# Attention's gate fourteen to seventeen steps later, the first merged set built in its output tiles, and a last pair of operands that is not sent to memory

## The chip, the cores and the metric

One core of a Trainium2 chip runs the whole layer. TensorE (PE) multiplies, VectorE (DVE) and ScalarE (ACT) work on the elements, GpSimd (POOL) and SyncE (SP) issue DMA transfers in their program's order. An engine runs its own list of instructions in order, and waits for others by semaphores. The metric is the device time of one execution in microseconds, the median of several; smaller is better.

## The reference

A bidirectional encoder layer on 768 tokens (512 and 256) of width 2048, all in float32. What is left out here are the modulation by `c`, the norms and the pooling windows.

```
proj = h @ w_in                       # 2048 -> 10240
pool_u, pool_z, q, k, v, attn_z, g_pool, g_attn = split(proj)
pool_y = _pool_mixer(pool_u) * silu(pool_z)
attn_y = _neighbourhood_attention(rms(q), rms(k), v, rpb) * silu(attn_z)   # the gate
merged = sigmoid(g_pool) * (pool_y @ w_pool_up) + sigmoid(g_attn) * (attn_y @ w_attn_up)
return x + gate * (merged @ w_o)
```

## The kernel before

Activations lie transposed: 128 features on the partitions, 768 tokens along the row, as a tile of 128 x 2 x 384 floats (384 KB). A weight or an activation is split in a rounded high part and the rest, and a product is three matmuls (high x high, high x low, low x high). Weights `wraw` are loaded by SP, split by ACT (`whi`, line 378) and DVE (`wlo`, line 379), three pieces ahead of PE.

Most products go by Strassen's scheme in Winograd's form: a *set* of activations (XA, XB, XR, XY, MA, MB, each with 4 *pairs* of tiles) is held as seven operands (B11, T1, T2, B21, T3, T4, B22) of each pair, and a *job* of seven products in 14 *steps* gives two output tiles `o1` and `o2` (line 490, 12 matmuls a product). A step is a place in the order in which the program is written, `clock["now"]`; everything that is not PE's main work is put into that order by `at(step, fn)`, or waits in one of three lists that `pump` serves once a step: `tasks` (loads that bring operands back), `back` (making a set's operands), `chores`.

`store` makes a set: `fetch` loads a pair of tiles (`in`) on SP, then `put` casts an operand on ACT (line 200) and subtracts on DVE (line 204), `differ` and `differ_too` make the differences on DVE (lines 284 to 290), and `save` sends an operand to memory on POOL (line 254). `recall` brings operands back on POOL (line 320). Operands named in `keep` stay. They lie in 46 slots of the slab, and `heap` counts those in use; a slot counts as free four steps after its save was issued, and who takes it next waits for the real landing. The tiles that jobs give lie in a ring of 7 buffers, the pool `outs`.

In the middle of the run eight pairs of heads go through attention beside the jobs of XB. A pair takes 42 steps, in six *units* of 7: scores, softmax, a transpose of the probabilities (`pt`, split by ACT into `ph` and by DVE into `pl`, line 697), and a product with v, whose tiles are transposed by PE first (`vt`, line 657). The gate, silu(attn_z), comes with the last unit: it loads `az`, takes exp, adds 1, takes log and exp again, and multiplies twice. The step is counted from the last unit's start, and the next pair starts 7 steps after that:

```python
stages += [(2, gate_load), (7, gate_exp), (8, gate_sum), (9, gate_log), (10, gate_inv), (12, gate_mul), (15, gated)]
```

After XB come eight jobs with XR (the pooled branch), eight with XY (attention, `au_done`), and eight each with MA and MB, the merged activations of features 0 to 1023 and 1024 to 2047, times `w_o`. In a job of XY each output tile is multiplied by its sigmoid gate `sig` (lines 962 to 966), gets the pooled branch added by an accumulating DMA (`o<-mp_d`, line 981), and goes to memory as `merged_d` (line 984). MA is made from `merged_d` while XY's jobs run, MB while MA's jobs run. In MA's jobs `x` is added by an accumulating DMA (line 995) and the sum goes to `half_d` (line 1001).

Of the kernel before, what the change touches and what calls it, by code (L numbers as in the profile page):

```python
# [44 lines left out]
PAIRS = 4  # L45
# [6 lines left out]
def encoder_layer(ctx: ExitStack, tc: tile.TileContext, xT, cT, w_ada2, w_ada4, b_ada, norm_g, w_in, pool_w,  # L52
# [37 lines left out]
    def release(t, n):  # L90
        if not any(t is o for o in outs.get("own", ())):
            after(n, free)

    def flat(t):
        return t.rearrange("p h n -> p (h n)")
# [48 lines left out]
    clock = {"now": 0}  # L144
# [48 lines left out]
    class Set:  # L193
# [3 lines left out]
        def put(self, op, j, src, then=None):  # L197

            t = self.ops[op, j] = slot(f"{self.name}{op}", F32R)
            act.copy(t[:, 0, :], src)  # L200
            flush()

            def rest():
                dve.tensor_tensor(t[:, 1, :], src, t[:, 0, :].bitcast(F32), op=ALU.subtract)  # L204
                if then is not None:
                    then()

            behind["fn"] = rest
            behind["of"] = t
# [30 lines left out]

    RAW = {"B11": ("a", 0), "B12": ("a", 1), "B21": ("b", 0), "B22": ("b", 1)}

    def store(st, load, ready=lambda j: True, make=None, last=None, keep=(), ahead=False):

        got = [{} for _ in range(st.pairs)]

        def fetch(j):
            got[j]["a"], got[j]["b"] = load(j)
            got[j]["t"] = clock["now"]

        def save(op, j):
            t = st.ops.pop((op, j))
            st.saved[op, j] = d = dram.tile([P, 2, TH], F32R, name=f"{st.name}{op}{j}")
            pool.dma_start(d, t)

            def landed():
                free()
                heap["flying"] -= 1
            after(4, landed)

        def put(op, j, src, then=None):
            kept = op in keep
            heap["flying"] += not kept

            def done():
                if then is not None:
                    then()
                if not kept:
                    save(op, j)

            st.put(op, j, src, done)
            mine = behind["of"]
            after(2, lambda: flush() if behind and behind["of"] is mine else None)

        def free_slot(op):
            return lambda: op in keep or heap["flying"] < heap["fly"] or hurry["on"]

        def here(j):
            return clock["now"] >= got[j]["t"] + 6 or hurry["on"]

        def differ(j):
            a, b = got[j]["a"], got[j]["b"]
            flush()
            dve.tensor_tensor(a[:, 0, :], a[:, 0, :], a[:, 1, :], op=ALU.subtract)
            dve.tensor_tensor(a[:, 1, :], b[:, 1, :], a[:, 1, :], op=ALU.subtract)

        def differ_too(j):
            a, b = got[j]["a"], got[j]["b"]
            dve.scalar_tensor_tensor(b[:, 1, :], a[:, 0, :], -1.0, b[:, 1, :], op0=ALU.mult, op1=ALU.subtract)
            dve.scalar_tensor_tensor(b[:, 0, :], b[:, 1, :], -1.0, b[:, 0, :], op0=ALU.mult, op1=ALU.subtract)  # L290

        def fetches(j):
            back.append((2, lambda: ready(j) and free_slot("")(), lambda: fetch(j)))

        def pair(j):
            if j == 0 or not ahead:
                fetches(j)
            if make is not None:
                for k in "ab":
                    back.append((0, lambda: here(j), lambda k=k: make(j, k, got[j][k])))  # L300
            for op in ("B22", "B21", "B11"):
                k, h = RAW[op]
                back.append((1, lambda op=op: here(j) and free_slot(op)(), lambda op=op, k=k, h=h: put(op, j, got[j][k][:, h, :])))
            back.append((0, lambda: True, lambda: differ(j)))
            back.append((0, lambda: True, lambda: differ_too(j)))
            if ahead and j + 1 < st.pairs:
                fetches(j + 1)
            for op, k, h, then in (("T3", "a", 1, None), ("T4", "b", 0, None), ("T1", "a", 0, free), ("T2", "b", 1, free)):
                back.append((1, free_slot(op), lambda op=op, k=k, h=h, then=then: put(op, j, got[j][k][:, h, :], then)))
            if j == st.pairs - 1 and last is not None:  # L310
                back.append((0, lambda: True, lambda: after(6, last)))

        for j in range(st.pairs):
            pair(j)

    def recall(st, keep=()):

        def load(op, j):
            t = st.ops[op, j] = slot(f"{st.name}{op}", F32R)
            pool.dma_start(t, st.saved[op, j])  # L320

        for op in ORDER:
            for j in range(0 if op not in keep else st.pairs, st.pairs):
                tasks.append((1, lambda op=op, j=j: (op, j) in st.saved, lambda op=op, j=j: load(op, j), 1))

    hurry = {"on": False}

# [271 lines left out]
    def attention(p, start, pace):  # L599
# [4 lines left out]
        def unit_(u):  # L604
# [148 lines left out]
            stages = [(-6, fetch), (0, scores), (1, biased), (3, exps), (5, vtrans), (6, vsplit), (5, recip), (6, norm),  # L753
                      (9, ptrans), (10, psplit), (13, values), (14, out)]
            if u == 5:
                stages += [(2, gate_load), (7, gate_exp), (8, gate_sum), (9, gate_log), (10, gate_inv), (12, gate_mul), (15, gated)]
            for d, fn in stages:
                if new or fn not in (vtrans, vsplit):
                    at(start + pace * u + d, fn)
# [218 lines left out]
    def au_done(f):  # L978
        def go(i, t):
            gate_with(16 + f, t)  # L980
            pool.dma_start(flat(t), mp_d[f], accum_op=ALU.add)

            def out():
                pool.dma_start(merged_d[f], flat(t))
                state.setdefault("merged", set()).add(f)
                release(t, 3)
            after(5, out)
        return go

# [230 lines left out]
    def stored(src, f):  # L1220
        got = []
        for i in range(2):
            t = slot("in")
            sp.dma_start(flat(t), src[f + i])
            got.append(t)
        return got

    with tc.tile_pool(name="attn", bufs=1, reuse_waits="tile") as at_:
        state["pool"] = at_
        act.preload_act_table_set(LNEXP)  # L1230
        now = clock["now"]
        first = now + 25
        for p in range(8):
            attention(p, first, 7 if p < DENSE else 8)
            first += 42 if p < DENSE else 56
        done = first + 14 - now
        heap["fly"] = 1
        store(XR, lambda j: stored(pooled_d, 2 * j))
        store(XY, lambda j: stored(attn_d, 2 * j), lambda j: state.get("gated", -1) >= 2 * j + 1)
        run(done)  # L1240
# [7 lines left out]
        sig_load(f)  # L1248
    recall(XY)
    run(14 + 14 * 8 + 2)  # L1250
    kept = ("B11", "T1", "T2")
    heap["gap"] = 2
    for k, st in enumerate((MA, MB)):
        store(st, lambda j, k=k: stored(merged_d, 8 * k + 2 * j),
              lambda j, k=k: {8 * k + 2 * j, 8 * k + 2 * j + 1} <= state.get("merged", set()), keep=kept, ahead=True)
        recall(st, kept)
        run(8 * 14)
    run(8 * 14 - 2)
# [91 lines left out]
```

## Time and profile before

| | |
|---|---|
| median of 3 runs | 2034.09 us (2033.81 to 2039.09) |
| the profiled execution | 2040.75 us, its span 2039.0 us |
| PE busy | 1925.6 us, 94% of the span |
| DVE, ACT, POOL busy | 66%, 51%, 19% |
| mean granted clock of TensorE | 0.972 |

The span runs from the first to the last instruction. PE works nearly all the time, so what a change is worth stands in the stretches where PE waits or runs at the lower of its two clock levels (1.2 in place of 2.4 GHz, a granted clock of 0.50). At the full clock PE does 232 matmuls of 384 columns in 40 us, 5.8 in a microsecond, so a job of 84 takes 14.5 us and a step 1.03 us.

### The profile page before, as it was taken

What the parts mean: (1) busy time and instruction counts of PE and PEld (TensorE: products, weight loads), DVE (VectorE), ACT (ScalarE), POOL (GpSimd) and SP (SyncE); (2) the same over time, 40 slices, a digit from 0 to 9 for tenths busy, and PEclk for the clock granted to TensorE, in tenths of its full rate; (3) what the DMA queues carried; (4) which work ended last, traced back from release to release, by engine and by line L of the source; (5) the groups of instructions that cost most, each with busy time, mean ns of one, the idle gap of its engine ahead of it and who ended that gap; (6) DMA issues with size and microseconds to landing.
All of it is one profiled execution on the core that took longest, in us unless ns stands there. A gap on an engine that the chain in (4) does not pass through costs nothing.

```text
span 2039.0 us, 32071 instructions
## 1 busy us (share of the span) xinstructions
PE 1925.6 (94%) x11752; PEld 1816.6 (89%) x11752; DVE 1354.6 (66%) x2422; ACT 1029.7 (51%) x2224; POOL 388.9 (19%) x617
## 2 busy tenths in 40 slices
PE   4899999999999999999999999999999997988997
PEld 2788889898999999999888988898999997888997
DVE  5755556666655588776687667777767776766654
ACT  4433334444434354456566666666545444554553
POOL 0000000111200256411111111111231222322311
PEclk8999999999999999999899999999999998989999
DMA  9755556887733645565656565556798789989965
GB/s 351 247 196 184 199 192 227 271 259 242 263 133 129 209 109 150 143 176 152 164 129 177 139 165 154 145 153 150 229 354 288 228 262 291 313 259 263 279 184 143
DMA packets 133774, 423.20 MB, mean 208 GB/s; under 512 B 16880, under 2 KB 22000, under 8 KB 133616
## 3 DMA queue, kind: packets, MB, share of 16 engines
q0 software_dynamic: 64352, 203.72, 36.5%
q1 hardware_dynamic: 68256, 217.35, 31.9%
q8 instruction: 92, 1.51, 0.3%
q14 instruction: 66, 0.54, 0.1%
q10 hardware_dynamic: 1008, 0.09, 0.0%
HBM read 296.83 MB, written 124.26 MB: 207 GB/s over the span
## 4 chain that ended last, share of the span: by engine, by line
PE 80%; DMA 6%; DVE 6%; issue 4%; ACT 3%; POOL 1%; SPq 0%; ACTq 0%; POOLq 0%; DVEq 0%
PE acc L490 69%; PE adaacc L527 2%; PE op L712 2%; PE acc L508 2%; DVE wlo L379 1%; PE n L553 1%; PE s L618 1%; DMA adaw<-in_w_ada_dram 1%; DMA maT<-maT 1%; PE pt L679 1%; DVE wsum L402 1%; DMA sig<-part_d 1%; PE yk L589 1%; DMA o<-mp_d 1%; DMA maB<-maB 1%
## 5 line engine op out<-in xcount | busy, mean ns | idle before, releaser
L379 DVE TENSOR_TENSOR wlo<-wraw,whi 128x512 fp32r<-128x512 f32 (+1 forms) x352 | 244.3, 695 | 320.0 <-ACT whi L378 312.4
L379 DVE TENSOR_TENSOR wlo<-wsum,whi 128x512 fp32r<-128x512 f32 x440 | 315.7, 718 | 127.2 <-ACT whi L378 119.3
L378 ACT CAST whi<-wsum 128x512 fp32r<-128x512 f32 x440 | 273.1, 621 | 158.6 <-ACT whi L378 54.9
L490 PE MATMUL acc<-xbT,whi 128*128 128x384 f32 x1280 | 345.8, 351 | 4.5 <-ACT u L417 4.5
L490 PE MATMUL acc<-xaT,whi 128*128 128x384 f32 x1216 | 313.4, 338 | 0.5 <-DVE xaT L204 0.5
L378 ACT CAST whi<-wraw 128x512 fp32r<-128x512 f32 (+1 forms) x352 | 212.9, 606 | 95.0 <-PE acc L490 75.9
L490 PE MATMUL acc<-xbB,whi 128*128 128x384 f32 x960 | 253.6, 345 | 1.7 <-DVE o L836 1.7
L417 ACT COPY u<-acc 128x384 f32<-128x384 f32 x220 | 105.2, 478 | 287.8 <-PE acc L490 287.6
L490 PEld LDWEIGHTS acc<-xbT,whi 128*128 128x128 f32 x1280 | 230.4, 193 | 12.7 <-ACT u L417 6.4
L490 PE MATMUL acc<-xaB,whi 128*128 128x384 f32 x912 | 235.3, 338 | 0.0
L490 PEld LDWEIGHTS acc<-xaT,whi 128*128 128x128 f32 x1216 | 217.6, 188 | 15.3 <-issue 13.6
L490 PE MATMUL acc<-xbT,wlo 128*128 128x384 f32 x640 | 219.6, 343 | 0.2 <-DVE wlo L379 0.2
L490 PE MATMUL acc<-xaT,wlo 128*128 128x384 f32 x608 | 203.7, 335 | 0.0
L490 PEld LDWEIGHTS acc<-xbB,whi 128*128 128x128 f32 x960 | 170.9, 190 | 8.6 <-issue 2.5
L490 PEld LDWEIGHTS acc<-xaB,whi 128*128 128x128 f32 x912 | 163.0, 188 | 11.9 <-issue 9.9
L490 PE MATMUL acc<-xbB,wlo 128*128 128x384 f32 x480 | 162.0, 338 | 0.0
L490 PE MATMUL acc<-xaB,wlo 128*128 128x384 f32 x456 | 152.8, 335 | 0.0
L402 DVE TENSOR_TENSOR wsum<-wraw 128x512 f32<-128x512 f32 x220 | 152.6, 694 | 0.0
L402 DVE TENSOR_TENSOR wsum<-wsum,wraw 128x512 f32<-128x512 f32 x220 | 151.4, 688 | 0.2
L849 POOL DMA_DIRECT2D part_d<-o x76 | 41.2, 542 | 442.8 <-ACT o L432 367.8
L490 PEld LDWEIGHTS acc<-xbT,wlo 128*128 128x128 f32 x640 | 123.5, 193 | 0.6 <-DVE wlo L379 0.6
L432 ACT ACTIVATE o<-acc 128x384 f32<-128x384 f32 x110 | 54.1, 491 | 119.6 <-PE acc L490 119.6
(240 smaller groups left out, 3597.0 us busy)
## 6 DMA issues: line engine op xcount, KB each, us to landing
wraw<-in_w_in_dram SPq DMA_DIRECT2D x160, 512.0 KB, 4.6
adaw<-in_w_ada_dram SPq DMA_DIRECT2D x96, 512.0 KB, 5.8
part_d<-o POOLq DMA_DIRECT2D x116, 384.0 KB, 4.3
wraw<-in_w_o_dram SPq DMA_DIRECT2D x32, 512.0 KB, 7.2
o<-part_d POOLq DMA_DIRECT2D x40, 384.0 KB, 5.0
xbT<-xbT POOLq DMA_DIRECT2D x32, 384.0 KB, 5.9
xrT<-xrT POOLq DMA_DIRECT2D x32, 384.0 KB, 6.9
xyT<-xyT POOLq DMA_DIRECT2D x32, 384.0 KB, 9.3
```

Of the source, the lines that this page charges most:

```text
L378: act.copy(hi[:, :n, :], raw)
L379: dve.tensor_tensor(lo[:, :n, :], raw, hi[:, :n, :].bitcast(F32), op=ALU.subtract)
L402: dve.tensor_tensor(t[:, :n, :], a, b, op=ALU.add)
L417: act.copy(t, c["a"][:, :TH])
L432: act.activation(c["o2"][:, 0, :], c["a"][:, :TH], AF.Copy, scale=-1.0)
L490: pe.matmul(out, w, m, start=s["first"] and j == 0 and k == 0, stop=j == n - 1 and k == 2, skip_group_check=True)
L508: pe.matmul(c["ps"][h], w[:, j, :], mov[h][m], start=s["begin"] and j == 0 and k == 0, stop=last and k == 2, skip_group_check=True)
L527: pe.matmul(acc[32 * j : 32 * (j + 1), :n], cs[:, kt, :], w[:, n * j : n * (j + 1)], start=kt == 0, stop=kt == KT - 1)
L553: pe.matmul(n2[:, 12 * i + 2 * u : 12 * i + 2 * u + 2], flat(c["s" + nm])[:, P * u : P * (u + 1)], blk1[:, 0:P:64], start=True, stop=True)
L589: pe.matmul(c["b"][HALF[h], u // 3, P * (u % 3) : P * (u % 3 + 1)], src, ident, start=True, stop=True)
L712: pe.matmul(op[:, :256], a, b, start=i == 0, stop=i == len(prods) - 1)
L849: pool.dma_start(part_d[f], flat(t))
```

## The change

Four things. The seven stages of the gate move from 2 to 15 steps behind the last unit's start to 16 to 32, which is 9 to 25 steps into the next pair; the stretch that runs with attention's pool becomes 17 steps longer (`done`), and the recall of XR's operands is listed after it. A set's operands are made 9 steps after a `fetch`, no longer 6. MA is made in the output tiles themselves: `au_done` notes tile `f` in `state["m", f]` for f < 8 and no longer sends it to `merged_d`, and MA's `load` returns these tiles. For f of 8 and more the tile still goes to `merged_d`, and counts as merged four steps after that. In MA and MB the operands of the last pair stay in their slots.

```diff
@@ store
-            kept = op in keep
+            kept = keep(op, j)
@@ here
-            return clock["now"] >= got[j]["t"] + 6 or hurry["on"]
+            return clock["now"] >= got[j]["t"] + (9 if own else 0) or hurry["on"]
@@ fetches, pair
+        gone = free if own else None
-            back.append((2, lambda: ready(j) and free_slot("")(), lambda: fetch(j)))
+            back.append((2 * own, lambda: ready(j) and free_slot("", j)(), lambda: fetch(j)))
@@ recall
-            for j in range(0 if op not in keep else st.pairs, st.pairs):
+            for j in range(st.pairs):
+                if not keep(op, j):
@@ attention
-                stages += [(2, gate_load), (7, gate_exp), (8, gate_sum), (9, gate_log), (10, gate_inv), (12, gate_mul), (15, gated)]
+                stages += [(16, gate_load), (21, gate_exp), (23, gate_sum), (24, gate_log), (26, gate_inv), (28, gate_mul), (32, gated)]
@@ au_done
             def out():
-                pool.dma_start(merged_d[f], flat(t))
-                state.setdefault("merged", set()).add(f)
-                release(t, 3)
+                if f < 8:
+                    state["m", f] = t
+                else:
+                    pool.dma_start(merged_d[f], flat(t))
+                    release(t, 3)
+                after(2 if f < 8 else 4, lambda: state.setdefault("merged", set()).add(f))
             after(5, out)
@@ the order of the stages
-        done = first + 14 - now
+        done = first + 31 - now
-    kept = ("B11", "T1", "T2")
+    kept = lambda op, j: op in ("B11", "T1", "T2") or j == PAIRS - 1
+    loads = (lambda j: [state["m", 2 * j], state["m", 2 * j + 1]], lambda j: stored(merged_d, 8 + 2 * j))
-        store(st, lambda j, k=k: stored(merged_d, 8 * k + 2 * j),
-              lambda j, k=k: {8 * k + 2 * j, 8 * k + 2 * j + 1} <= state.get("merged", set()), keep=kept, ahead=True)
+        store(st, loads[k], lambda j, k=k: {8 * k + 2 * j, 8 * k + 2 * j + 1} <= state.get("merged", set()), keep=kept,
+              ahead=True, own=k == 1)
```

The lines of the changed kernel are 3 to 7 higher than those of before (379 is 382, 697 is 700). The order of PE's instructions is the same in both. First, DVE where the second pair of heads begins, in the kernel before: from the split of v (`vs`) to the split of the first unit's probabilities (`pl`); `in` are the store's differences, `o<-o,az` is the last step of the gate.

```order
L672 TENSOR_TENSOR vs<-vt,vs 64x128
L284 TENSOR_TENSOR in<-in 128x384
L285 TENSOR_TENSOR in<-in 128x384
L379 TENSOR_TENSOR wlo<-wraw,whi 128x512
L747 TENSOR_TENSOR o<-o,az 128x768
L627 SCALAR_TENSOR_TENSOR p<-s,ny,bias 128x256 x2
L630 TENSOR_REDUCE mx<-p 128x2
L289 SCALAR_TENSOR_TENSOR in<-in 128x384
L290 SCALAR_TENSOR_TENSOR in<-in 128x384
L402 TENSOR_TENSOR wsum<-wsum,wraw 128x512
L379 TENSOR_TENSOR wlo<-wraw,whi 128x512
L697 TENSOR_TENSOR pl<-pt,ph 128x256
```

The same place on DVE now, up to the same `pl`.

```order
L675 TENSOR_TENSOR vs<-vt,vs 64x128
L382 TENSOR_TENSOR wlo<-wraw,whi 128x512
L630 SCALAR_TENSOR_TENSOR p<-s,ny,bias 128x256 x2
L633 TENSOR_REDUCE mx<-p 128x2
L405 TENSOR_TENSOR wsum<-wsum,wraw 128x512
L382 TENSOR_TENSOR wlo<-wraw,whi 128x512
L700 TENSOR_TENSOR pl<-pt,ph 128x256
```

The gate's last product and the four differences no longer stand ahead of `pl`. From one `pl` to the next there were 22 instructions here and are 16; at the other six starts of a pair there were 17 to 20, and there are 15 or 16, but at the sixth pair 20, where the store's four differences come to stand now. Then DVE up to the next unit's `pl`, in the kernel before.

```order
L672 TENSOR_TENSOR vl<-vt,vh 128x128
L402 TENSOR_TENSOR wsum<-wsum,wraw 128x512
L379 TENSOR_TENSOR wlo<-wsum,whi 128x512
L204 TENSOR_TENSOR xrT_10171<-in,xrT_10171 128x384
L627 SCALAR_TENSOR_TENSOR p<-s,ny,bias 128x256 x2
L630 TENSOR_REDUCE mx<-p 128x2
L379 TENSOR_TENSOR wlo<-wsum,whi 128x512
L697 TENSOR_TENSOR pl<-pt,ph 128x512
```

The same place now; `ez` is the gate's sum.

```order
L675 TENSOR_TENSOR vl<-vt,vh 128x128
L405 TENSOR_TENSOR wsum<-wsum,wraw 128x512
L382 TENSOR_TENSOR wlo<-wsum,whi 128x512
L630 SCALAR_TENSOR_TENSOR p<-s,ny,bias 128x256 x2
L633 TENSOR_REDUCE mx<-p 128x2
L289 SCALAR_TENSOR_TENSOR in<-in 128x384
L290 SCALAR_TENSOR_TENSOR in<-in 128x384
L382 TENSOR_TENSOR wlo<-wsum,whi 128x512
L736 TENSOR_SCALAR ez<-ez 128x768
L700 TENSOR_TENSOR pl<-pt,ph 128x512
```

The gate's sum and two of the differences have come here (the other two stand some rows further up), and the gate's two products follow in the next two units. Last, SP while XY's jobs run, in the kernel before: `in<-merged_d` are MA's loads, `sig` the gates', `wraw` the weights'.

```order
L962 DMA sig<-part_d_182 128x768
L962 DMA sig<-part_d_181 128x768
L1224 DMA in<-merged_d_227 128x768
L1224 DMA in<-merged_d_228 128x768
L356 DMA wraw<-in_w_au_dram 128x1024 x2
L962 DMA sig<-part_d_184 128x768
L962 DMA sig<-part_d_183 128x768
L356 DMA wraw<-in_w_au_dram 128x1024
L1224 DMA in<-merged_d_229 128x768
L1224 DMA in<-merged_d_230 128x768
L356 DMA wraw<-in_w_au_dram 128x1024
```

SP at the same place now.

```order
L965 DMA sig<-part_d_182 128x768
L965 DMA sig<-part_d_181 128x768
L359 DMA wraw<-in_w_au_dram 128x1024 x2
L965 DMA sig<-part_d_184 128x768
L965 DMA sig<-part_d_183 128x768
L359 DMA wraw<-in_w_au_dram 128x1024 x2
```

MA's eight loads are gone from between the weights and the gates. On POOL 24 transfers are gone: eight of `merged_d`, and for MA and MB together eight saves and eight recalls.

## Rows read from the trace of the kernel before

**Rows 1.** The page's line of busy time, share of the span and instructions.

```profile
PE 1925.6 (94%) x11752; PEld 1816.6 (89%) x11752; DVE 1354.6 (66%) x2422; ACT 1029.7 (51%) x2224; POOL 388.9 (19%) x617
```

**Rows 2.** PE's waits, whole run: who for whom, us in total, times, longest.

```profile
PE acc L490 <- ACT u L417: 23.6, 13, 10.9
PE vt L657 <- DVE pl L697: 20.7, 16, 3.6
```

**Rows 3.** Windows of pairs two to seven in attention; engines' busy us, clock, DMA, GB/s.

```profile
938.40:1011.10 72.70, 68.33 (x401) 62.34 (x400) 50.10 (x105) 44.63 (x120) 9.21 (x13) 0.91 0.56 147
...
1078.80:1145.20 66.40, 63.92 (x400) 58.66 (x400) 48.74 (x104) 44.55 (x119) 8.63 (x12) 0.97 0.60 156
...
sum 414.30, PE 393.87 PEld 360.58 DVE 295.69 ACT 265.47 POOL 54.62; mean PE 65.64 PEld 60.10 DVE 49.28 ACT 44.25 POOL 9.10
...
980.50:987.30 6.80, 6.80 (x25) 5.69 (x24) 4.26 (x10) 2.61 (x8) 0.53 (x1) 0.50 0.52 178
```

**Rows 4.** PE's waits at the start of the fourth pair, 1090 to 1130 us.

```profile
PE vt L657 <- DVE pl L697: 1.6, 1, 1.6
```

**Rows 5.** Timeline of PE at the start of the second pair: start, us, what, idle before.

```profile
979.09 0.30 PE L657 MATMUL vt<-ident,o 128*128 128x128 f32 x1 [3.47 <-DVE pl L697]
```

**Rows 6.** Timeline of DVE ahead of that wait.

```profile
968.57 0.95 DVE L742 TENSOR_TENSOR az<-az,ez 128x768 f32<-128x768 f32 x1
...
973.56 0.95 DVE L747 TENSOR_TENSOR o<-o,az 128x768 f32<-128x768 f32 x1
...
975.94 0.55 DVE L289 SCALAR_TENSOR_TENSOR in<-in 128x384 f32<-128x384 f32 x1
```

**Rows 7.** DVE's waits in the unit after, 979 to 992 us.

```profile
DVE pl L697 <- ACT ph L692: 2.0, 1, 2.0
DVE wlo L379 <- ACT whi L378: 1.6, 1, 1.6
```

**Rows 8.** Windows of 40 us, from XY's jobs to MA's; columns as in group 3.

```profile
1640.00:1680.00 40.00, 38.54 (x216) 36.90 (x216) 29.50 (x49) 20.71 (x40) 9.43 (x14) 1.00 0.77 230
1680.00:1720.00 40.00, 29.08 (x153) 28.76 (x152) 25.36 (x44) 17.15 (x33) 8.12 (x13) 0.83 0.95 285
1720.00:1760.00 40.00, 35.09 (x187) 34.45 (x187) 31.80 (x55) 20.81 (x41) 10.44 (x16) 0.91 0.97 290
1760.00:1800.00 40.00, 33.16 (x165) 30.26 (x164) 22.97 (x39) 16.38 (x31) 13.44 (x23) 0.87 1.05 336
1800.00:1840.00 40.00, 40.00 (x232) 39.84 (x231) 31.57 (x57) 25.96 (x53) 12.02 (x18) 1.00 0.85 235
1840.00:1880.00 40.00, 32.42 (x174) 30.87 (x173) 24.20 (x45) 18.56 (x39) 10.70 (x17) 0.91 0.90 258
```

**Rows 9.** Waits of SP's queue, 1640 to 1800 us.

```profile
SPq L1224 <- DMA merged_d<-o: 28.0, 2, 18.3
...
SPq L962 <- DMA maT<-maT: 8.4, 1, 8.4
```

**Rows 10.** Timeline of ACT, 1679 to 1697 us.

```profile
1691.03 0.51 ACT L200 CAST maB<-in 128x384 fp32r<-128x384 f32 x1 [11.22 <-DMA in<-merged_d]
```

**Rows 11.** Chain that ended last, 1733 to 1748 us: start, us, what.

```profile
1734.50 5.66 DMA maT<-maT
...
1740.28 5.26 DMA sig<-part_d
```

**Rows 12.** DMA view of 1640 to 1800 us.

```profile
DMA packets 14791, 45.66 MB, mean 285 GB/s; under 512 B 1761, under 2 KB 1761, under 8 KB 14781
```

**Rows 13.** Timeline of ACT in MA's jobs, 1852 to 1867 us.

```profile
1865.70 0.51 ACT L200 CAST mbB<-in 128x384 fp32r<-128x384 f32 x1 [10.66 <-DMA mbT<-mbT]
```

**Rows 14.** Window in which XR's operands come back; columns as in group 3.

```profile
1463.00:1525.00 62.00, 62.00 (x360) 62.00 (x359) 40.34 (x69) 29.39 (x54) 25.64 (x43) 1.00 1.12 356
```

**Rows 15.** DMA issues of 1512 to 1514.8 us: count, KB, median us to landing.

```profile
xrB<-xrB POOLq DMA_DIRECT2D x2, 384.0 KB, 9.1
```

**Rows 16.** Timeline of PE, where the last recalled XR operand is first read.

```profile
1528.89 0.51 PE L490 MATMUL acc<-xrB,whi 128*128 128x384 f32 x2
```

More of the change, by code (lines that the diff above doesn't have):

```diff
@@ L241, in encoder_layer, with store @@
     RAW = {"B11": ("a", 0), "B12": ("a", 1), "B21": ("b", 0), "B22": ("b", 1)}
-    def store(st, load, ready=lambda j: True, make=None, last=None, keep=(), ahead=False):
+    def store(st, load, ready=lambda j: True, make=None, last=None, keep=lambda op, j: False, ahead=False, own=True):
         got = [{} for _ in range(st.pairs)]
@@ L273, in put, with free_slot @@
             after(2, lambda: flush() if behind and behind["of"] is mine else None)
-        def free_slot(op):
-            return lambda: op in keep or heap["flying"] < heap["fly"] or hurry["on"]
+        def free_slot(op, j):
+            return lambda: keep(op, j) or heap["flying"] < heap["fly"] or hurry["on"]
         def here(j):
-            return clock["now"] >= got[j]["t"] + 6 or hurry["on"]
+            return clock["now"] >= got[j]["t"] + (9 if own else 0) or hurry["on"]
         def differ(j):
@@ L302, in pair @@
                 k, h = RAW[op]
-                back.append((1, lambda op=op: here(j) and free_slot(op)(), lambda op=op, k=k, h=h: put(op, j, got[j][k][:, h, :])))
+                back.append((1, lambda op=op: here(j) and free_slot(op, j)(), lambda op=op, k=k, h=h: put(op, j, got[j][k][:, h, :])))
             back.append((0, lambda: True, lambda: differ(j)))
@@ L307, in pair @@
                 fetches(j + 1)
-            for op, k, h, then in (("T3", "a", 1, None), ("T4", "b", 0, None), ("T1", "a", 0, free), ("T2", "b", 1, free)):
-                back.append((1, free_slot(op), lambda op=op, k=k, h=h, then=then: put(op, j, got[j][k][:, h, :], then)))
+            for op, k, h, then in (("T3", "a", 1, None), ("T4", "b", 0, None), ("T1", "a", 0, gone), ("T2", "b", 1, gone)):
+                back.append((1, free_slot(op, j), lambda op=op, k=k, h=h, then=then: put(op, j, got[j][k][:, h, :], then)))
             if j == st.pairs - 1 and last is not None:
@@ L314, in store, with recall @@
             pair(j)
-    def recall(st, keep=()):
+    def recall(st, keep=lambda op, j: False):
         def load(op, j):
@@ L322, in recall @@
         for op in ORDER:
-            for j in range(0 if op not in keep else st.pairs, st.pairs):
-                tasks.append((1, lambda op=op, j=j: (op, j) in st.saved, lambda op=op, j=j: load(op, j), 1))
+            for j in range(st.pairs):
+                if not keep(op, j):
+                    tasks.append((1, lambda op=op, j=j: (op, j) in st.saved, lambda op=op, j=j: load(op, j), 1))
     hurry = {"on": False}
```

## The prediction

> **What bounds the kernel now.** I read the page's busy line first: PE is busy 1925.6 us of a span of 2039.0, DVE 66% and ACT 51% [rows 1]. So PE is the bound as a whole, its order is the same in both kernels, and a gain can only come from two things: time in which PE waits, and time at the clock of 0.50 that follows a wait. The waits of PE, grouped by who waits for whom, come next. Two groups lead: the products `acc` that wait for ACT's split of a weight (`u`, 23.6 us, one wait of 10.9), and the transposes of v that wait for DVE's `pl` (20.7 us, up to 3.6 each) [rows 2]. The third view is windows cut at the starts of the pairs and every 40 us later, in which the reader is to compare the number of matmuls with 5.8 in a microsecond; that gives a loss for each stage, idle time and clock together. Three stages that the change touches lose: attention [rows 3], XY's jobs as they end and MA's as they begin, and MA's later jobs [rows 8].
>
> **Attention.** A pair's period has the same work each time. In the first window shown PE is busy 68.33 us at a mean clock of 0.91; 18% of 72.7 us, that is 13.1, were at 0.50, and half of these are lost, which leaves 61.8. In the other it is 63.92 at 0.97: 4.0 us slow, 2.0 lost, 61.9 [rows 3]. With some 0.5 us that PE waits in every period for other things I take 62.4. Six periods take 414.3 us [rows 3] in place of 374.4, so 39.9 are lost.
>
> How much of that is the gate's? Every start of a pair has one wait of `vt` for `pl`. At the second pair it is 3.47 us [rows 5], and the 6.8 us right behind it run at 0.50 [rows 3], which costs another 3.4. DVE shows why: just ahead of this `pl` it makes the gate's two products, 0.95 us each, and the store's four differences, 0.55 each [rows 6]. These are 4.1 us, and the wait is 3.5. The fourth pair's wait was 1.6 us [rows 4]; its period, the other one in [rows 3], loses 66.4 - 62.4 = 4.0, so 2.4 are not the gate's. Taking 2.4 for each of six periods as what stays, 39.9 - 14.4 = 25.5 hang on the wait. The seventh start, outside these windows, adds its 3.6 [rows 2] and half of some 3.4 slow microseconds: 5.3. At most 31 are to be had.
>
> What the move adds: the same instructions now stand one to four units later. There DVE has gaps. In the unit after the wait it idles 2.0 us for `ph` and 1.6 for a weight's high part [rows 7], and more in shorter waits. The gate's three DVE operations (0.95 twice [rows 6], and a sum over the same row without a second operand, at most 0.95) are spread over three units, so a unit gets 0.6 to 1.9 us where 3.6 and more are idle. That is the cover; if it were gone, each of six pairs would lose up to 1.9 us. I charge 0.8 a pair, 5 in all. The sixth pair keeps its load (20 instructions, where the four differences come to stand), so I keep a wait of 2.4 and half of a slow stretch there, 4 in all. **Term 1: 31 - 4 - 5 = 22.** Bounds: 31 if all goes, 5 if DVE's lag merely moves to the next `pl`.
>
> **The recall of XR.** It begins 17 steps later, and XY's last seven saves are now in it. By the order the last of XR's recalls is issued 3 steps, 3.1 us, later than before. Before, the recalls around it landed 9.1 us after their issue [rows 15], that one at 1522, and PE reads the operand first at 1528.9 [rows 16]: a margin of 6.8, now some 3.7. By bytes: 28 recalls, 7 saves and 2 loads of 0.393 MB are 14.5 MB; weights (two of 0.524) and outputs (two of 0.393) of four and a half jobs add 8.2; 22.8 MB at the 356 GB/s of [rows 14] take 64 us, from 1463 to 1527, 2 us before the need. I charge nothing, with a narrow margin. The Trainium skill, "DMA: Bandwidth & Descriptors", section Bandwidth, gives 425 GB/s for a 16 MB load by one core whose neighbour idles; the estimate from that page is 54 us and a margin of 12. The window's row is the one I go by, since it has this kernel's mix of sizes and directions.
>
> **MA in place.** From 1640 to 1800 PE did 721 matmuls [rows 8], which are 124.3 us at 5.8: 35.7 lost. The cause starts at SP. MA's loads `in<-merged_d` stand in its queue and wait 28.0 us for the merged tiles to land, one of them 18.3 [rows 9]; weights and gates queue behind them. ACT in turn stands 11.22 us at the cast of `maB` until that load lands [rows 10], and the split of PE's weight stands behind this cast: that is the 10.9 of [rows 2]. The clock falls behind it: 0.83, 0.91 and 0.87 in the three windows [rows 8]. In the new kernel neither the write, nor the landing, nor the load exists for MA; the cast reads the output tile, and the order puts its operands at about the same steps. A second knot is at 1734: a `sig` load (5.26 us) waits for the save of a `maT` whose slot it takes (5.66) [rows 11], SP standing 8.4 [rows 9]. It stays in part, as that slot is still reused, five steps later than before.
>
> DMA: 45.66 MB went through in those 160 us, 285 GB/s [rows 12]. Twenty-four transfers less are 9.4 MB; 36.2 MB remain, and in 124 us that is 292 GB/s, under the 336 that one of these windows reached [rows 8], so transfers do not set the end. DVE has 109.6 us of work there (25.36 to 31.80 a window, [rows 8]), 88% of 124.3: tight. New hazards: output tiles are held until the casts have read them, in a ring of 7. By the order only the second tile of the sixth MA job comes close, since it takes the buffer of a merged tile whose write is issued five steps earlier; DVE may wait 2 to 5 us there. The eight recalls left come in one burst. I keep 8 of the 35.7. **Term 2: 27.5.** Bounds: 14 if half of it is DVE's and POOL's, 35.7 if all goes.
>
> **MB, last pair kept.** From 1840 to 1880 PE did 174 matmuls, 30.0 us of work: 10.0 lost [rows 8]. ACT stands 10.66 us at the cast of `mbB` for the landing of the save whose slot it takes [rows 13]; POOL is late with that save, as its queue holds recalls that wait for saves and accumulating transfers. In the new order the same reuse is there, and until then only transfers that come later are gone. MB's load is asked four steps later, which keeps SP free. I keep 6 of 10. **Term 3: 4.** Bounds: -5 (the four steps are late next) to 10.
>
> **Sum.** 22 + 27.5 + 4 less 1 for small waits at the gate's exps and log on ACT = 52.5. The profiled execution is 2040.75 us, 6.66 above the median of 2034.09; 2040.75 - 52.5 = 1988.3, and less 6.66 the forecast is 1982.
>
> **Rivals.** (A) DVE lags at the starts of pairs for other reasons, and `pl` waits one unit on. For it: DVE is busy 49 of 69 us of a period, and `pl` still has 15 to 20 instructions ahead. Against: the wait is about as long as what is taken away. Term 1 falls to 5: 1999. (B) MA's stage keeps half of its loss, through DVE's 88% or the ring of 7, where PE's drain of `acc` into `o` waits for a buffer. Term 2 falls to 14: 1995.5. (C) Several at once, MB's later load included: term 1 of 10, term 2 of 14, term 3 of -1: about 2010. (D) Nothing takes the place of the waits: 31 + 35.7 + 10 = 76.7, so 1957. For it: PE has windows of 40.00 busy at clock 1.00 right beside these [rows 8]. (E) The other side: XR's operands come late. If the queues gave 157 GB/s there, about what the windows of attention move (147 and 156, [rows 3]), the recall would take 145 us and end at 1608, 79 after PE's need at 1529: 2034 - 52.5 + 79, about 2060. It decides where the recall ends more than 52.5 us late, in 118 us, which is below 193 GB/s. Against it stands the row of 356. (F) The waits are only handed to others and the time stays within 0.3%, about what a measurement of this kernel can tell from no change.
>
> **How the numbers follow.** Forecast 0.57, A 0.13, B 0.12, C 0.05, D 0.08, E 0.03, F 0.02. The forecast, A and B hold 0.82; with the bounds of the terms (a few us below 1982 where term 1 or 2 reaches its end, 2005 where A or B is a little worse) the range is 1964 to 2005. Faster by over 0.3%: all but E and F, 0.95; slower 0.03.
>
> **What would show it.** Right: `vt` waits for `pl` at the sixth pair alone, about 2.4 us; periods of a pair of about 65 us; no SP wait on `merged_d` ahead of MA; no wait of 11 us at `maB`; and PE near 232 matmuls in most 40-us windows of XY's and MA's jobs. The wait of `mbB` for a save remains. Wrong: waits of `vt` or `av` for `pl` in a pair's second to fourth unit (A); `acc` waiting for DVE's `o`, and that for a `merged_d` write (B); PE waiting for a DMA `xr` after 1500 (E).

## The result, and the profile after

| | before (4 runs) | after (4 runs) |
|---|---|---|
| median | 2033.95 us (2029.72 to 2039.09) | 2000.97 us (1995.99 to 2003.67) |
| profiled execution, span | 2040.75, 2039.0 us | 1998.88, 1997.1 us |
| mean granted clock | 0.972 | 0.982 |

The changed kernel takes 0.9834 of the time before, with an interval of 0.9802 to 0.9865. The forecast was 1982 in a range of 1964 to 2005: the direction and the range hold, the gain is 33 us in place of 52.

Where it came from can be read without any guess, since PE's order is the same: one takes the same PE instruction in both traces and subtracts its starts. This lead of the changed kernel, at times of the kernel before, is 2.8 us at 100, 1.2 at 890, 19.4 at 1440, 11.3 at 1600, 11.3 at 1640, 39.9 at 1817, and 40.0 at 1900 and at PE's last products; the spans differ by 41.9. So attention gained 18.2, XR's first job lost 8.1, XY's and MA's jobs gained 28.6, and MB's part of them 0.1.

The page's busy line and PE's waits of the changed kernel, which answer to [rows 1, 2]:

```profile
PE 1910.8 (96%) x11752; PEld 1805.7 (90%) x11752; DVE 1353.2 (68%) x2422; ACT 1028.5 (52%) x2224; POOL 375.6 (19%) x593
```

```profile
PE acc L493 <- ACT u L420: 13.1, 8, 8.0
...
PE vt L660 <- DVE pl L700: 6.8, 17, 1.0
PE acc L493 <- DVE o L432: 6.0, 1, 6.0
PE acc L493 <- DMA xrT<-xrT: 3.4, 2, 2.1
```

The transposes of v wait 6.8 us where they waited 20.7. New are a wait for DVE's `o` and waits for XR's operands (3.4 us for `xrT`, and 1.9 for `xrB` further down the list). Attention's periods, from one wait ahead of the norms to the next (start:end, us, busy us of PE, PEld, DVE, ACT and POOL, clock, DMA share, GB/s), answer to [rows 3]:

```profile
937.10:1004.60 67.50, 65.65 (x401) 60.04 (x400) 48.93 (x104) 44.14 (x119) 8.59 (x12) 0.95 0.55 142
...
1137.20:1202.60 65.40, 64.10 (x400) 58.60 (x400) 48.92 (x104) 43.66 (x118) 8.67 (x12) 0.97 0.61 158
1202.60:1269.40 66.80, 64.22 (x401) 58.60 (x400) 49.68 (x105) 44.21 (x120) 9.19 (x13) 0.97 0.62 161
...
sum 399.50, PE 389.40 PEld 355.60 DVE 293.24 ACT 263.55 POOL 52.81; mean PE 64.90 PEld 59.27 DVE 48.87 ACT 43.92 POOL 8.80
```

Six periods take 399.5 us in place of 414.3. The quietest is no shorter than 65.4: the slow clock stays. The same columns for windows of 40 us answer to [rows 8, 14]:

```profile
1440.00:1480.00 40.00, 40.00 (x233) 40.00 (x232) 29.62 (x50) 17.83 (x35) 14.30 (x24) 1.00 1.00 298
1480.00:1520.00 40.00, 34.65 (x186) 32.54 (x186) 20.62 (x34) 16.20 (x29) 16.50 (x28) 0.96 1.12 358
...
1640.00:1680.00 40.00, 40.00 (x233) 40.00 (x232) 36.09 (x62) 24.26 (x47) 7.92 (x12) 1.00 0.86 253
1680.00:1720.00 40.00, 34.02 (x188) 33.70 (x187) 30.16 (x52) 21.57 (x42) 10.81 (x16) 0.91 0.88 249
1720.00:1760.00 40.00, 40.00 (x232) 39.91 (x232) 32.46 (x56) 21.97 (x42) 10.50 (x17) 1.00 0.99 287
1760.00:1800.00 40.00, 40.00 (x233) 40.00 (x232) 33.67 (x63) 27.18 (x55) 12.70 (x20) 1.00 0.92 290
1800.00:1840.00 40.00, 30.52 (x162) 29.21 (x161) 23.30 (x43) 18.31 (x37) 11.26 (x18) 0.91 0.92 247
```

Counted in matmuls against 232, three dips are left: 46 missing at 1480 (XR's operands late), 44 at 1680 and 70 at 1800. The last two have one pattern, seen on POOL. Its timeline at the first, in the changed kernel:

```profile
1692.75 0.89 POOL L984 DMA_DIRECT2D o<-mp_d  x1 [1.76 <-DVE o L969]
1693.32 0.87 POOL L254 DMA_DIRECT2D maB<-maB  x1
1699.78 0.55 POOL L322 DMA_DIRECT2D maB<-maB  x1 [5.59 <-DMA maB<-maB]
1700.31 0.93 POOL L984 DMA_DIRECT2D o<-mp_d  x1
1700.88 0.93 POOL L990 DMA_DIRECT2D merged_d<-o  x1
```

A save of `maB` (line 254) is followed by the recall of the same operand (line 322), which must wait for the save to land: POOL stands 5.59 us, and the second accumulation is late by that, and with it the write of `merged_d` behind it. DVE's `o` needs the buffer that this write reads, and gets it when the write has landed (the chain that ended last):

```profile
1700.88 9.80 DMA merged_d<-o
```

PE stands until then (its timeline):

```profile
1711.41 1.01 PE L493 MATMUL acc<-xyB,whi 128*128 128x384 f32 x2 [5.98 <-DVE o L432]
```

At 1820 POOL stands again for its own save, and ACT, behind it, for the save of an `mbT` whose slot it takes:

```profile
1809.62 0.87 POOL L254 DMA_DIRECT2D mbB<-mbB  x1
1819.93 0.55 POOL L322 DMA_DIRECT2D mbB<-mbB  x1 [9.44 <-DMA mbB<-mbB]
```

```profile
1831.18 0.51 ACT L200 CAST mbB<-in 128x384 fp32r<-128x384 f32 x1 [5.90 <-DMA mbT<-mbT]
```

A third wait of this kind, 7.19 us at 1679, cost PE nothing. And the recall of XR, POOL's timeline where it begins:

```profile
1450.64 0.85 POOL L858 DMA_DIRECT2D part_d<-o  x1 [4.73 <-ACT o L435]
1451.19 0.87 POOL L322 DMA_DIRECT2D xrB<-xrB  x1
...
1453.34 1.99 POOL L322 DMA_DIRECT2D xrB<-xrB  x3
```

The theory from these rows has three parts. (1) The gate's move pays in attention, but starts the recall too late, which takes back 8.1. (2) MA in place pays by the transfers that fell away. (3) What is left in MA's and MB's stages is POOL waiting with a recall for its own save. The rivals are told with each run.

### The profile page after: what moved, and what is told of

It is laid out like the page before. It is cut to its first block, busy times and chain, and to the rows that moved or that the text cites. A ratio compares the mean times of both kernels' runs of the same rounds, so it can differ in the third digit from the quotient of the medians.

```text
span 1997.1 us, 31988 instructions
## 1 busy us (share of the span) xinstructions
PE 1910.8 (96%) x11752; PEld 1805.7 (90%) x11752; DVE 1353.2 (68%) x2422; ACT 1028.5 (52%) x2224; POOL 375.6 (19%) x593
## 4 chain that ended last, share of the span: by engine, by line
PE 83%; DVE 5%; DMA 4%; issue 3%; ACT 3%; POOL 1%; SPq 0%; ACTq 0%; POOLq 0%; DVEq 0%
PE acc L493 73%; PE adaacc L530 2%; PE op L715 2%; PE acc L511 1%; DVE wlo L382 1%; PE n L556 1%; DMA adaw<-in_w_ada_dram 1%; PE s L621 1%; PE pt L682 1%; DMA xrB<-xrB 1%; PE yk L592 1%; DVE wsum L405 0%; DMA merged_d<-o 0%; DMA mbB<-mbB 0%; ACT o L435 0%
## 5 line engine op out<-in xcount | busy, mean ns | idle before, releaser
L493 PEld LDWEIGHTS acc<-xaT,whi 128*128 128x128 f32 x1216 | 217.7, 188 | 15.3 <-issue 14.4
```

The lines of the kernel that those rows point to most:

```text
L493: pe.matmul(out, w, m, start=s["first"] and j == 0 and k == 0, stop=j == n - 1 and k == 2, skip_group_check=True)
```

## The experiments

All runs are compared with the kernel before on the same chip; the median of the changed kernel, 2001, is the mark. The kernel before had medians of 2031.6 beside E1 to E4, 2035.4 beside E5 to E8 and 2034.2 beside E9 to E11, so between such groups the ratios are the safer comparison. The gains by stage are the differences of the lead described above, each from one profile.

| run | attention (890 to 1440) | XR (1440 to 1600) | XY, MA (1640 to 1817) | MB (1817 to 1900) | median us | ratio to before |
|---|---|---|---|---|---|---|
| the change | 18.2 | -8.1 | 28.6 | 0.1 | 2001.0 | 0.983 |
| E1 gate back | 3.8 | 0.0 | 28.5 | 0.0 | 2002.3 | 0.985 |
| E2 recall early | 15.4 | -14.6 | 29.0 | -0.2 | 2006.8 | 0.988 |
| E3 MA from memory | 22.0 | -7.4 | 13.6 | -0.6 | 2015.1 | 0.991 |
| E4 last pair not kept | 17.4 | -10.2 | 20.8 | 0.2 | 2015.9 | 0.991 |
| E5 last gate old | 18.4 | 0.0 | 28.7 | -0.2 | 1992.2 | 0.979 |
| E6 recall after 10 steps | 19.5 | -10.5 | 33.2 | 12.4 | 1983.7 | 0.975 |
| E8 gate alone | 11.7 | -6.6 | 0.3 | 0.4 | 2027.8 | 0.997 |
| E9 E5 and E6 | 18.5 | 0.0 | 33.3 | 12.3 | 1973.5 | 0.970 |
| E11 E9, B21 kept | 15.3 | 0.0 | 36.2 | 12.3 | 1973.3 | 0.970 |

E7 and E10 change PE's order and are told below. Attention's column differs by up to 6.7 us between kernels whose attention is the same (the change, E3 to E6, E9, E11), and XR's by 3.1 (the change, E3, E4, E6). These differences go with the time at a clock of 0.50 that each profile happened to have: from 930 to 1440 us it is 27.2 us in E3, 37.4 in E9 and 44.2 in E11. So a difference of a few microseconds there means nothing in one profile. The column of XY and MA agrees to 0.5 us where the edits there are the same (28.5 to 29.0; 33.2 and 33.3). The runs behind one median lie up to 13 us apart.

**E1.** The gate and the recall go back.

```diff
-                stages += [(16, gate_load), (21, gate_exp), ... (32, gated)]
+                stages += [(2, gate_load), (7, gate_exp), ... (15, gated)]
-        done = first + 31 - now
+        done = first + 14 - now
```

> The changed kernel with the gate's seven stages and the recall of XR put back to their old steps; the other parts stay. Aligned by PE's instructions, the changed kernel gained 16.7 us in attention and lost 8.1 at XR's first job. Theory: both hang on the gate's move, so undoing it costs 16.7 - 8.1 = 8.6 us: about 2009.5 against 2001; waits of vt for pl sum to about 20 us, and PE waits for no xr operand. Rival 1: the late XR operands come from elsewhere; then they stay late and it costs 16.7, about 2018. Rival 2: attention's gain is within what one profile varies; then the time is 1993 without the loss at XR.

Measured: 2002.3 us (1998.9 to 2005.6), ratio 0.9847 [0.9824, 0.9871]. The median moved by 1 where 8.6 was expected, the profiled span by 6.7 (2003.8 against 1997.1). PE's waits in this kernel:

```profile
PE vt L660 <- DVE pl L700: 18.5, 16, 3.5
```

The waits of `vt` are back, and no wait for XR is left in the list. By stage, the gate's move is worth 18.2 - 3.8 = 14.4 in attention (the expectation's 16.7 counts the change's lead from 880 us, not 890) and costs 8.1. Rival 1 falls, since no XR operand is late. The medians alone do not tell the theory from rival 2; the whole move with its recall was worth 1.3 by them. E5 decides, since it differs from this kernel only in the gates of the first seven pairs: 2002.3 against 1992.2, 10.1 us by the medians and some 12 by the ratios, with attention at 18.4 in place of 3.8. So rival 2 falls too.

**E2.** Only the recall goes back to its old place, while the last pair's gate is still to come.

```diff
         done = first + 31 - now
...
+        at(first + 14, lambda: (heap.update(spare=1, fly=3), recall(XR)))
         run(done)
...
-    heap.update(spare=1, fly=3)
-    recall(XR)
```

> The changed kernel with the gate where the change put it, but the recall of XR listed 17 steps earlier, where it was before the change. Theory: the recall's bytes take 64 us at 356 GB/s and only started too late; PE then waits for no xr operand and 8.1 us come back: about 1993 against 2001. Rival: the queue and the transfers of attention's end are the limit, the operands stay late or attention's own saves and loads are late in their place: 2001 or more.

Measured: 2006.8 us (2005.7 to 2012.6), ratio 0.9878 [0.9856, 0.9900]. The theory's remedy failed and the rival was right: the last pair's `attn_d` now stands behind eleven recalls on POOL, XY's load waits for it, and ACT's cast stands, as its timeline shows.

```profile
1465.62 0.51 ACT L200 CAST xyB<-in 128x384 fp32r<-128x384 f32 x1 [11.53 <-DMA in<-attn_d]
```

PE then waits 7.3 us for ACT, and later still 3.2 us for `xrB`. It is not enough to begin the recall sooner; the write that XY needs must come sooner too.

**E3.** MA is made from memory again.

```diff
-                if f < 8:
-                    state["m", f] = t
-                else:
-                    pool.dma_start(merged_d[f], flat(t))
-                    release(t, 3)
-                after(2 if f < 8 else 4, ...)
+                pool.dma_start(merged_d[f], flat(t))
+                release(t, 3)
+                after(0 if f < 8 else 4, ...)
...
-              ahead=True, own=k == 1)
+              ahead=True, own=True)
```

> The changed kernel with MA made from memory again: all sixteen merged tiles are written, MA's are loaded; the gate's move, the kept last pair and the four later steps for MB stay. Theory: the 28.5 us between 1640 and 1830 come from the write, the landing and the load that fell away, so it costs 28: about 2029 against 2001, with SP waiting over 20 us for merged tiles and ACT some 10 us at maB. Rival: the gain came from the transfers that the kept last pair takes away; then it costs under 10, 2001 to 2010.

Measured: 2015.1 us (2009.7 to 2022.6), ratio 0.9914 [0.9891, 0.9937]: 14 us lost, between the two expectations. SP waits again for merged tiles (its queue's waits, 1620 to 1800 us):

```profile
SPq L1227 <- DMA merged_d<-o: 23.2, 3, 8.4
```

The longest of these is 8.4 where it was 18.3 [rows 9]. So about half of the stage's gain, 28.6 - 13.6 = 15.0, needs MA in place, beside a last pair that is kept (MA's operands are made 9 steps after the load here, where the kernel before had 6). The other 13.6 came with MA still in memory; E4 takes one more piece out.

**E4.** The last pair is saved and recalled.

```diff
-    kept = lambda op, j: op in ("B11", "T1", "T2") or j == PAIRS - 1
+    kept = lambda op, j: op in ("B11", "T1", "T2")
```

> The changed kernel with the last pair of MA and MB saved and recalled as before. Theory: keeping it was worth nothing at MB (0 us by the alignment) and little at MA: 2001 to 2005. Rival, the forecast's own term: 4 us at MB and some of MA's gain: 2006 to 2012.

Measured: 2015.9 us (2008.4 to 2019.0), ratio 0.9910 [0.9885, 0.9934]. Neither expectation held: it costs about 15 us. By stage 7.8 of it is in XY's and MA's jobs, where PE again waits for recalled operands (its waits, 1640 to 1860 us):

```profile
PE acc L493 <- DMA maB<-maB: 2.4, 3, 2.0
PE acc L493 <- DMA maT<-maT: 2.3, 4, 1.3
```

At MB nothing changed, as the alignment had it. The profiled span is 14.6 longer than the changed kernel's: the other 6.8 lie in front of XY's jobs (2.1 of them at XR) and behind PE's last products, where the edit does nothing. So 7.8 is what the profile shows for the kept last pair, and why the medians differ by 15 stays open.

**E5.** The last pair's gate alone at its old steps, with the recall.

```diff
-                stages += [(16, gate_load), ... (32, gated)]
+                stages += list(zip((2, 7, 8, 9, 10, 12, 15) if p == 7 else (16, 21, 23, 24, 26, 28, 32),
+                                   (gate_load, gate_exp, gate_sum, gate_log, gate_inv, gate_mul, gated)))
-        done = first + 31 - now
+        done = first + 14 - now
```

> The changed kernel with the gate of the last pair alone at its old steps (there is no next pair whose pl it could delay), and with it the recall of XR listed 17 steps earlier, as before the change. Moving the recall alone had put the last pair's attn_d write behind eleven recalls in POOL's queue. Theory: the seven starts of a pair stay without their waits, the write is early, the recall starts at its old place, and the 8.1 us at XR's first job come back: a span of about 1989 against 1997.1 in the profile, and a median of about 1993; PE waits for no xr operand. Rival: attention's end and the recall share the transfers however they are listed, the time stays at 2001 or above.

Measured: 1992.2 us (1988.5 to 1995.1), ratio 0.9789 [0.9773, 0.9805], span 1987.8: the theory's numbers. The windows of this kernel show the dip closed, with transfers at 367 GB/s:

```profile
1480.00:1520.00 40.00, 40.00 (x232) 40.00 (x232) 25.31 (x41) 20.18 (x36) 15.12 (x27) 1.00 1.12 367
```

So the loss at XR hung on the recall's start and on the last pair's write together. The last pair's gate never needed to move, since no `pl` of a next pair stands behind it.

**E6.** In MA and MB a recall waits until ten steps after its save.

```diff
-    def recall(st, keep=lambda op, j: False):
+    def recall(st, keep=lambda op, j: False, lag=0):
...
-                    tasks.append((1, lambda op=op, j=j: (op, j) in st.saved, ...
+                    tasks.append((1, lambda op=op, j=j: (op, j) in st.saved and (hurry["on"] or clock["now"] >= st.when[op, j] + lag), ...
...
-        recall(st, kept)
+        recall(st, kept, 10)
```

> The changed kernel where in MA and MB an operand is recalled no earlier than 10 steps after its save was issued. In the changed kernel B21's recall stands right behind its save on POOL and waits 5.6 us (near 1694) and 9.4 us (near 1810) for it to land. Theory: this makes the merged write late, for which DVE's o and PE wait 6.0 us at 1705, and the save for which ACT's cast and PE wait 8.0 us at 1825; without it both go, and the slow clock behind them: 10 to 20 us, a median of 1981 to 1991. Rival: the accumulating transfers on POOL (7.3 us each to land) set these times alone; then 2001.

Measured: 1983.7 us (1980.4 to 1986.5), ratio 0.9747 [0.9734, 0.9761]: 17 us gained by this edit alone. PE's waits of this kernel from 1690 to 1840 us are all that is left of the two dips:

```profile
PE acc L495 <- ACT u L422: 1.0, 1, 1.0
PE acc L495 <- DMA maB<-maB: 0.9, 3, 0.4
```

From 1640 to 1900 us POOL waits as long for accumulations to land before it writes a merged tile as in the changed kernel (first line; the second is E6's):

```profile
POOL merged_d L990 <- DMA o<-mp_d: 26.6, 7, 8.9
POOL merged_d L992 <- DMA o<-mp_d: 24.5, 8, 10.1
```

No recall waits for its own save any more in that stretch, so what made the accumulations late was the recall ahead of them. The third part of the theory is shown.

**E7.** The 24 products of two columns for the norms, in two halves with main products between.

```diff
-(2, sums), (3, take), (4, root), ...
+(2, sums), (3, lambda: half(1, "q")), (4, take), (5, root), ...
```

> The changed kernel with the 24 two-column products of a pair's norms split in two halves one step apart, with main products between (the rest of the norms one step later; PE's order changes). In the changed kernel each stretch at the clock of 0.50 in attention begins 2 to 5 us behind these 24 products (3.3 us with the wait ahead of them) and none behind the waits of vt of 0.43. Theory: the 24 in a row are what the clock falls for; split, the eight slow stretches (40.8 us, half of it lost) go for the most part: 10 to 20 us, a median of 1981 to 1991. Rival: the clock falls for the small products of attention as a whole; the stretches stay, 2001.

Measured: 1993.3 us (1982.0 to 2001.6), ratio 0.9791 [0.9766, 0.9816]. The runs lie 20 us apart, too far for the question; E10 asks it again.

**E8.** The kernel before, with the gate's stages and `done` of the change and nothing else.

```diff
-                stages += [(2, gate_load), ... (15, gated)]
+                stages += [(16, gate_load), ... (32, gated)]
-        done = first + 14 - now
+        done = first + 31 - now
```

> The kernel before with the gate's move and the later recall of XR alone. Theory, from the sum of the parts: 14.5 us gained in attention, 8.1 lost at XR's first job, nothing else: 6.4 faster, about 2026 beside 2031.5 to 2034 of before. Rival 1: the loss of XR's first job hangs on the other parts, then 14.5 faster, 2018. Rival 2: the gate's move changes later stages too (the loss of 35.7 us in MA's stage then differs by over 5 us).

Measured: 2027.8 us (2024.7 to 2037.6), ratio 0.9972 [0.9958, 0.9987]; the span is 4.1 shorter than before's. Attention gains 11.7, XR loses 6.6, and later stages move by less than 1. The first theory holds, and both rivals fall. It also shows that XY's and MA's jobs gain nothing from the gate (0.3): with E3 and E4 the 28.6 are 15.0 that need MA in place, 7.8 that need the last pair kept, and some 5.8 that either brings, or that come with the waiting of 9 steps and MB's four, which no run tried apart.

**E9.** E5's and E6's edits together.

> The changed kernel with two of the edits tried before together: the last pair's gate at its old steps (with the recall of XR), and in MA and MB no recall sooner than 10 steps after its save. Theory: the two work at different places, so the gains of their spans add: 1997.1 - 9.3 - 15.8 = 1972, a median of about 1974. Rival: they draw on the same slack; then about that of the better one, 1983.

Measured: 1973.5 us (1970.6 to 1977.7), ratio 0.9703 [0.9679, 0.9726], span 1974.8. The gains add. It beats the changed kernel by 27 us.

**E10.** E9 with E7's edit.

> The kernel with the two edits together, and the 24 small products of the norms in two halves one step apart. Alone the split gave a median of 1993 between 1982 and 2002, which settled nothing. If the 24 in a row are what the clock falls for, the slow time in attention (34 to 41 us without the split) falls to under 20 us and the median to about 1966. Rival: the clock falls for something else near them; slow time and median stay, about 1974.

Measured: 1975.0 us (1963.3 to 1979.4), ratio 0.9702 [0.9672, 0.9732]; no gain by the medians. The clock over attention, 880 to 1420 us, in the changed kernel:

```profile
880.00:1420.00 540.00, 528.13 (x3250) 484.70 (x3251) 396.65 (x832) 351.23 (x940) 71.89 (x102) 0.96 0.60 156
```

in E9:

```profile
880.00:1420.00 540.00, 528.33 (x3258) 484.87 (x3258) 396.92 (x832) 352.66 (x943) 72.67 (x102) 0.96 0.61 156
```

and in E10:

```profile
880.00:1420.00 540.00, 527.01 (x3277) 483.35 (x3275) 400.61 (x839) 355.55 (x949) 73.44 (x103) 0.97 0.61 157
```

Added up from 930 to 1440 us, the time at a clock of 0.50 is 37.4 us in E9 and 27.2 in E10, as in E7. But the kernels with the gate moved and the 24 products in a row have 27.2 (E3) to 47.6 (E8), so that is no more than their own variation. The slow stretches do not go, nor do they fall under the 20 us that the theory asked for. Whether the split helps stays open.

**E11.** E9, with B21 of every pair kept.

```diff
-    kept = lambda op, j: op in ("B11", "T1", "T2") or j == PAIRS - 1
+    kept = lambda op, j: op in ("B11", "T1", "T2", "B21") or j == PAIRS - 1
```

> The kernel with the two edits together, and B21 of every pair of MA and MB kept instead of saved and recalled, with the same count of slots in use: 12 transfers less. If what is left in MA's and MB's stages (PE near full there) hangs on transfers, 1 to 3 us faster than without, about 1972; the other theory, that nothing there waits for B21 once its recall no longer stands behind its save: no change, about 1974, or worse where the next operand's recall takes the slots sooner.

Measured: 1973.3 us (1973.1 to 1974.7), ratio 0.9700 [0.9675, 0.9724]. The medians cannot tell it from E9. The stage can: XY's and MA's jobs gain 36.2 in place of 33.3, the 1 to 3 us of the first theory, where equal kernels agree to 0.5. Two windows of E9:

```profile
1680.00:1720.00 40.00, 39.04 (x225) 38.73 (x225) 35.74 (x62) 23.25 (x47) 9.41 (x14) 1.00 0.98 297
1720.00:1760.00 40.00, 39.38 (x223) 38.19 (x222) 31.24 (x54) 21.90 (x43) 13.24 (x21) 1.00 0.96 274
```

and the same of E11:

```profile
1680.00:1720.00 40.00, 40.00 (x233) 40.00 (x232) 37.49 (x65) 25.34 (x50) 8.37 (x12) 1.00 0.95 272
1720.00:1760.00 40.00, 40.00 (x232) 40.00 (x231) 31.24 (x54) 22.12 (x44) 12.97 (x21) 1.00 0.95 273
```

PE has no wait left there. Attention alone varies by more than 2.9 us from one profile to the next, so medians that agree do not show that the twelve transfers are worth nothing.

## Why the prediction was right and where it was off

**The bound and the places** were right: what was won in the stages named came from PE's waits and the slow clock there, and the waits of `vt`, ACT's 11 us at `maB` and SP's 28 us are gone or down to a third.

**Term 1** (22) measured 18.2, and 15.3 to 22.0 in the profiles of kernels with the same attention, so the number alone settles little. The waits fell by 13.9 us, and no new wait over 1.0 came up, so rival A is out, and the sixth pair, for which 4 were kept, waits 0.99. What was mis-sized is what stays: the step took the fourth pair's 2.4 us above 62.4 for every period. Without the gate's wait the six periods are still 399.5 / 6 = 66.6, so 4.2 above, 10.8 us in six. That the term came so near is luck in part: the 9 us held back for DVE's lag and the sixth pair were hardly needed, and made up for it. Most of the 4.2 is the clock, 0.95 to 0.97 in each of these windows: at a mean of 0.96, 0.04 of 66.6 us, 2.7, are lost. One of its slow stretches (window of the changed kernel):

```profile
1007.80:1011.20 3.40, 3.40 (x13) 2.95 (x12) 1.38 (x6) 0.91 (x3) 1.34 (x2) 0.50 0.65 147
```

It begins 2.8 us behind the start of the norms' 24 products (PE's timeline):

```profile
1005.01 2.84 PE L556 MATMUL n<-blk,sq 128*128 128x2 f32 x24 [0.42 <-ACT sq L550]
```

The forecast put the time at 0.50 down to waits. In the kernel before, from 930 to 1440 us, it was 51.0 us: 20.4 at waits of `vt` for `pl`, and 30.6 behind these 24 products, a place that the change leaves alone. In the changed kernel nothing is left of the first, and 37.4 stand behind the products.

**The recall** (0) measured -8.1, and this is the step that failed. Its 22.8 MB at 356 GB/s gave 64 us, and that held:

```profile
1453.00:1517.00 64.00, 59.07 (x327) 56.96 (x325) 39.23 (x67) 27.75 (x52) 27.03 (x47) 0.97 1.11 351
```

351 GB/s for 64 us is 22.5 MB. The Trainium skill's 425 GB/s in "DMA: Bandwidth & Descriptors", section Bandwidth, stands there for one load of 16 MB, and this mix of sizes and directions did not reach it: by an estimate from that page the same bytes would have been in 11 us sooner, and no operand late. What was wrong is the start. The forecast had it at 1463; it came at 1453 of the changed kernel, which is 1453 + 19.4 = 1472 on the clock of before. That is 9 later, so a margin of 2 to 4 us became a lack of 5 to 7: PE waits 5.3 us for XR's operands, and a slow stretch of 3.4 follows. The recall began behind a write of `part_d` for which POOL waited 4.73 us for ACT: its place in the program's order does not tell when POOL gets to it. Rival E was this mechanism with a far too large price; it should have had a small one with a real chance. E5 showed that the price is avoidable.

**Term 2** (27.5) measured 28.6, by the way described: no merged tile for SP to wait for, no cast held up. The split of it (15.0 in place, 7.8 the last pair) was not foreseen; the forecast had put the whole down to the first, so that the sum came out to 1 us is luck in part. The second knot did not shrink: SP stands 13.4 us for a `maT` where it stood 8.4, but no wait of PE hangs on it. The hazard named for the second tile of MA's sixth job, 2 to 5 us, came as 6.0 with a slow stretch behind it, but in XY's sixth job (`acc<-xyB` at 1711): the buffer of a merged tile is taken there, and the forecast named the wrong set. E6 shows that it is not the ring of output buffers that is too short, but the write that is late.

**Term 3** (4) measured 0.1. That the reuse of the saved slot would stay was foreseen. The working said itself that only transfers that come later are gone, and took 4 of the 10 all the same, without a row for it. POOL stood 9.44 us for its own save. Such waits, which the working names, were there before the change too (31.5 us of POOL in five, 1640 to 1920 us), and the change left three. E6 gave 12.4 there, about all that the stage had lost (10.0 from 1840 to 1880, and 1.9 in the 30 us behind).

**Sum.** By terms: 22 - 1 + 0 + 27.5 + 4 = 52.5 forecast. Measured are 18.2 - 8.1 + 28.6 + 0.1 = 38.8, and 3.1 more (41.9 - 38.8) outside these stages: 1.2 in front of attention and 1.9 behind PE's last products. The medians differ by less than the profiles, since before's profiled execution was 6.8 above its median and the changed kernel's 2.1 below: 41.9 - 8.9 = 33.0. So of the 19 us that the gain fell short, 10.6 lie in the profile's terms and the rest in which executions were profiled. The forecast took before's 6.7 above the median to stay, and it did not. Rival A's time, 1999, is near the measured one, but its mechanism did not occur.

## What to carry to other kernels

A transfer that reads back what the same queue has just written waited in the queue here, 5.6 to 9.4 us, and what stood behind it was late. Leave some steps between the two: ten, about 10 us, were enough for landings of 6 to 10 us and gave 17 us by one condition; no other number was tried. When work is moved later, look at the last round by itself: what follows there is another stage, and the move may give back in it what the other rounds won. When a total cannot tell two kernels apart, compare them stage by stage. And a transfer's start is to be counted from its queue, with its waits, not from the step at which the program lists it.

## What the runs showed of the hardware

The slow clock in attention was not tied to the length of PE's waits alone. Waits of `vt` of 0.43 to 0.99 us in the changed kernel were followed by no slow stretch. The norms' wait of 0.42 with 24 two-column products behind it, 3.3 us in all, was followed by one of 3.4 us in the case shown, and splitting the products in two moved the mean clock over attention from 0.96 to 0.97 only (E9 and E10, one profile each), within what equal kernels vary. Transfers in both directions reached 351 to 367 GB/s over 40 to 64 us, with the 16 DMA engines' share shown at 1.11 to 1.12.
